# Output product of a hybrid trunk: the short convolution's second 1024 tokens through seven block products

## The chip, the cores and the metric

The program runs on one core of one Trainium2 chip. The metric is device time in microseconds of one execution of the whole kernel; less is better.

## The reference, cut to what matters

One layer over 2048 tokens of width 1024, in float32. A normalised input goes through one projection to six parts; two mixers read them; their outputs, side by side, go through one output projection `w_out` of 2048 by 1024; then an MLP follows.

```python
h = rmsnorm(x, norm_mix_w)
u_b, u_c, u_h, z, xbc, dt_raw = split(h @ w_in)          # 1024 columns each, xbc 1536, dt_raw 16
y_a = u_b * causal_dwconv(u_c * u_h, short_conv_w)       # short convolution, width 3
y_b = ssd_mixer(z, xbc, dt_raw, ...)                     # chunked state-space scan, gate, grouped norm
x = x + concat([y_a, y_b], -1) @ w_out                   # w_out: 2048 x 1024
h = rmsnorm(x, norm_mlp_w)
x = x + square(relu(h @ w_up)) @ w_down
out = rmsnorm(x, final_norm_w)
```

## The kernel before, in words

**Layout and precision.** Activations lie with features on the 128 partitions and tokens along the row. A token block is 512 tokens (`TB`), so the 2048 tokens are blocks 0 to 3; a half is 1024 tokens, two blocks. Each float32 operand is cut into a high and a low part (`uh`, `ul` for activations, `whi`, `wlo` for weights), and each product is three matmuls, high by high, high by low and low by high. A main matmul is 128 by 128 weights on 512 tokens.

**Seven products.** A product of a 2 by 2 block matrix of weights with a 2 by 2 block matrix of activations (two blocks of features by two blocks of tokens) needs eight block products the plain way, and seven with sums and differences of blocks taken first. `chain` (L267) does such a product for two column tiles of 128 outputs and one half of the tokens: seven products named b11, t1, t2, b21, t3, b22, t4, each of 4 feature tiles by 3 matmuls, 84 main matmuls in all, into three accumulators px, py and pw. Such a run is called a pair here. `after(name)` is called behind each product; it is where other work is put beside the pair. The sums of weights for the next pair are made by `combine` (L244) on VectorE; where the same columns are used for both halves, the sums of the first use are stored in DRAM and loaded at the second. The sums of activations are made where the activations come out, and are read back as seven blocks per feature tile (`land` L349, `part` L355: load into the `ul` tile, copy the high part to `uh` on ScalarE, subtract on VectorE).

**Second half** (`second_half`, L1039). Pairs 20 to 41 are the second half's input projection (`LATER`, 22 pairs; pairs 0 to 19 are the first half's). Pairs 42 to 45 (`OUTS`, o0 to o3) are the output projection of the short convolution's first half of tokens, blocks 0 and 1: y_a's seven blocks come from `y7_d`. In pair 41 the activations of the input projection are exchanged for these (`renew`), and in pair 42 the rest of them is (`renew_rest`).

**Plain units** (`Output`, L1722). The rest of the output projection is done the plain way in 48 units of one token block by one column tile, 8 feature tiles by 3 matmuls, 24 main matmuls each, accumulator pm. Pass 1 (units 0 to 15) is y_a for blocks 2 and 3, read from `ys_d`; passes 2 and 3 are y_b for blocks 0 and 2, then 1 and 3. Each unit adds its residual (`xt`, loaded from `x` in pass 1 and from `x1_d` afterwards) and stores to `x1_d`.

**The scan.** `Scan` (L1491) works through 32 chunks of 128 tokens and 8 heads. A chunk's inputs come by DMA (`load` L1518: bc, xd, dec; `load_rows`: eb; `load_gate`: y). `front` starts with TensorE transposes of xd into ptx; `back` has TensorE products st, yo, yd, then pss, and a string of VectorE steps. `run` is a generator of eight steps for a chunk, and `after` and `hook` take steps from it: chunks 0 to 21 (`SPLIT` 22) beside pairs 20 to 45, with one buffer for each chunk tile, one step behind each product, but only two steps in pair 41 and two in pair 42 (`LIGHT`); chunks 22 to 31 beside the units, with two buffers and three steps for each unit.

**Order.** On each engine, and on SP's DMA queue, instructions run in the order of the built program. A scheduler at build time sets this order from the code; nearly all DMAs are issued from SP. A transpose on TensorE whose xd has not landed holds up all matmuls behind it.

Of the kernel before, what the change touches and what calls it, by code (L numbers as in the profile page):

```python
# [16 lines left out]
P = 128  # L17
# [22 lines left out]
def trunk(ctx: ExitStack, tc: tile.TileContext, x, x_tok, w_in, w_dt, w_out, w_up, w_down, cvec, hrow, out):  # L40
# [22 lines left out]
    ys_d = dram.tile([P, 8, TH], F32, name="ys_d")  # L63
    y7_d = [dram.tile([P, 7, TB], F32, name=f"y7_d{k}") for k in range(4)]
# [147 lines left out]
    class Seven:  # L212
# [158 lines left out]
        def prepare(self, h, src, base, accs=None, held=None):  # L371
# [32 lines left out]
            for k in range(4):  # L404
                ts = [held("nb") if held and i == 1 else self.raw("nb") for i in range(4)]
# [15 lines left out]
                if held:  # L421
                    self.held.append(ts[1])
                    nc.sync.dma_start(self.stored[h][k][:, 4:6], ts[2])
# [30 lines left out]
    class Proj(Seven):  # L454
# [6 lines left out]
        OUTS = "o0 o1 o2 o3".split()  # L461
# [381 lines left out]
        def pair(self, h, what, ws, ahead, after):  # L843
# [33 lines left out]
            def evict(name, gi, pm):  # L877
# [17 lines left out]
                elif name == "b22":  # L895
# [4 lines left out]
                    elif kind == "b":  # L900
                        mul(to["c12"], to["c12"], self.cc[n][:, hi])
                        if h:
                            nc.sync.dma_start(ys_d[:, n], a)
                        else:
                            nc.sync.dma_start(y7_d[n][:, 0], to["c11"])
                            s["t13"], s["t24"] = self.e("t13"), self.e("t24")
                            self.sub(s["t13"][:, lo], to["c12"], to["c11"])
                            self.sub(s["t13"][:, hi], to["c22"], to["c12"])
                            self.sub(s["t24"][:, lo], to["c22"], s["t13"][:, lo])
                            nc.sync.dma_start(y7_d[n][:, 1:5:3], s["t13"].rearrange("p (a t) -> p a t", a=2))  # L910
# [7 lines left out]
                elif kind == "b":  # L918
                    mul(to["c21"], pm["x"], self.cc[n + 4][:, lo])
                    if h:  # L920
                        nc.sync.dma_start(ys_d[:, n + 4], b)
                    else:
                        nc.sync.dma_start(y7_d[n][:, 3:6:2], b.rearrange("p (a t) -> p a t", a=2))
                        self.sub(s["t24"][:, hi], to["c21"], s["t24"][:, lo])
                        nc.sync.dma_start(y7_d[n][:, 2:7:4], s["t24"].rearrange("p (a t) -> p a t", a=2))
# [9 lines left out]
        def residual(self, n, b):  # L935
# [3 lines left out]
            nc.sync.dma_start(t.rearrange("p (a t) -> p a t", a=2), x[b, :, 2 * n : 2 * n + 2])  # L939

        def out_pair(self, n, ws, ahead, after):
# [4 lines left out]
            def evict(name, gi, pm):  # L946
# [10 lines left out]
                if fin:  # L957
                    nc.sync.dma_start(x1_d[b][:, 2 * n + i], t)
# [3 lines left out]
        def renew(self, name):  # L962

# [1027 lines left out]
```

## Time and profile before

| | |
|---|---|
| median of 3 runs | 2608.24 us (2600.61, 2608.24, 2608.95) |
| profiled execution, its own time | 2602.47 us |
| its span, first to last instruction | 2600.5 us |
| TensorE busy | 2581.2 us of the span, 99% |
| VectorE busy | 1918.2 us, 74% |
| ScalarE busy | 1398.9 us, 54% |
| granted TensorE clock, mean | 0.999 |

Main matmuls overlap, so a row's mean duration (some 390 ns) is longer than the distance from one start to the next; what a matmul costs in a row of matmuls is read from a stretch divided by its count. In a row of the windows view stand, in this order: the stretch (us from the span's start), its length, and the busy time with the count of instructions in brackets for TensorE's matmuls, TensorE's weight loads, VectorE, ScalarE and GpSimd, then the granted TensorE clock, the DMA engines' share and GB/s. All rows are of the one profiled execution.

### The profile page before, as it was taken

How to read it: one execution, taken by the hardware profiler on the slowest of the kernel's cores; microseconds unless marked ns; L12 is line 12 of the kernel's file. 1: busy time of each engine (PE TensorE's matmuls, PEld its weight loads, DVE VectorE, ACT ScalarE, POOL GpSimd, SP SyncE). 2: the span in 40 equal slices, each digit the busy share in tenths (PEclk: the TensorE clock that was granted, in tenths of full speed). 3: DMA queues.
4: the chain of work that ended last, by engine and by line, in shares of the span. 5: the costliest groups of instructions: out<-in, count | busy, mean ns of one | idle time of the engine just before them, and what ended most of it. 6: DMA issues, size and time to landing. Idle time of an engine off the chain costs nothing.

```text
span 2600.5 us, 33553 instructions
## 1 busy us (share of the span) xinstructions
PE 2581.2 (99%) x12018; PEld 2125.3 (82%) x12018; DVE 1918.2 (74%) x2634; ACT 1398.9 (54%) x2178; POOL 65.3 (3%) x97
## 2 busy tenths in 40 slices
PE   9999999999999999999999999999999999999999
PEld 7888888788888787788888888888888888888887
DVE  7988766777777888877777765755558877877875
ACT  7554345766566865645336555655456444444443
POOL 0011000000000000000000000000000000000001
PEclk9999999999999999999999999999999999999999
DMA  5557545555555577987665674744448766676872
GB/s 214 203 206 275 199 145 190 173 170 180 163 158 185 176 255 258 281 268 234 206 220 200 238 267 142 252 161 142 161 142 283 259 205 208 222 241 219 281 251 77
DMA packets 291655, 540.23 MB, mean 208 GB/s; under 512 B 25888, under 2 KB 142112, under 8 KB 291488
## 3 DMA queue, kind: packets, MB, share of 16 engines
q1 hardware_dynamic: 291056, 537.70, 61.2%
q8 instruction: 94, 1.54, 0.2%
q14 instruction: 73, 0.60, 0.1%
q10 hardware_dynamic: 432, 0.39, 0.0%
HBM read 358.17 MB, written 179.83 MB: 207 GB/s over the span
## 4 chain that ended last, share of the span: by engine, by line
PE 70%; DMA 4%; DVE 3%; ACT 3%; issue 1%; SPq 0%; DVEq 0%; ACTq 0%
PE px L292 11%; PE px L293 11%; PE px L294 11%; PE py L292 5%; PE py L293 5%; PE py L294 5%; PE pm L132 3%; PE pm L134 3%; PE pm L133 3%; PE pw L292 3%; PE pw L293 3%; PE pw L294 3%; DMA dec<-rd_d 1%; DMA xd<-xs_d 1%; PE yd L1621 1%; PE yo L1618 1%
## 5 line engine op out<-in xcount | busy, mean ns | idle before, releaser
L292 PE MATMUL px<-uh,whi 128*128 128x512 f32 x1736 | 680.7, 392 | 2.6 <-ACT pw L300 1.5
L293 PE MATMUL px<-ul,whi 128*128 128x512 f32 x1736 | 676.3, 390 | 0.0
L294 PE MATMUL px<-uh,wlo 128*128 128x512 f32 x1736 | 675.7, 389 | 0.0
L292 PEld LDWEIGHTS px<-uh,whi 128*128 128x128 f32 x1736 | 325.9, 188 | 75.7 <-ACT pw L300 2.3
L294 PEld LDWEIGHTS px<-uh,wlo 128*128 128x128 f32 x1736 | 325.9, 188 | 68.1
L293 PEld LDWEIGHTS px<-ul,whi 128*128 128x128 f32 x1736 | 326.1, 188 | 65.7
L109 DVE TENSOR_TENSOR wlo<-wraw,whi 128x1024 fp32r<-128x1024 f32 (+1 forms) x224 | 224.8, 1003 | 193.9 <-ACT whi L108 189.9
L108 ACT CAST whi<-s 128x1024 fp32r<-128x1024 f32 (+1 forms) x214 | 223.9, 1046 | 229.9 <-PE py L293 85.2
L292 PE MATMUL py<-uh,whi 128*128 128x512 f32 x868 | 339.4, 391 | 0.0
L293 PE MATMUL py<-ul,whi 128*128 128x512 f32 x868 | 337.9, 389 | 0.0
L294 PE MATMUL py<-uh,wlo 128*128 128x512 f32 x868 | 337.9, 389 | 0.0
L108 ACT CAST whi<-wraw 128x1024 fp32r<-128x1024 f32 (+1 forms) x224 | 196.2, 876 | 245.7 <-PE px L293 168.9
L109 DVE TENSOR_TENSOR wlo<-s,whi 128x1024 fp32r<-128x1024 f32 (+1 forms) x214 | 260.4, 1217 | 73.3 <-ACT whi L108 72.1
L292 PEld LDWEIGHTS py<-uh,whi 128*128 128x128 f32 x868 | 163.0, 188 | 34.3 <-DVE state L1637 0.5
L294 PEld LDWEIGHTS py<-uh,wlo 128*128 128x128 f32 x868 | 162.9, 188 | 34.0
L293 PEld LDWEIGHTS py<-ul,whi 128*128 128x128 f32 x868 | 163.0, 188 | 33.3
L132 PE MATMUL pm<-uh,whi 128*128 128x512 f32 (+1 forms) x456 | 175.9, 386 | 0.0
L348 DVE TENSOR_TENSOR ul<-rh,uh 128x1024 fp32r<-128x1024 f32 (+1 forms) x128 | 139.0, 1089 | 49.9 <-ACT uh L347 49.8
L134 PE MATMUL pm<-uh,wlo 128*128 128x512 f32 (+1 forms) x456 | 174.0, 382 | 0.0
L133 PE MATMUL pm<-ul,whi 128*128 128x512 f32 (+1 forms) x456 | 173.4, 380 | 0.0
L347 ACT CAST uh<-rh 128x1024 fp32r<-128x1024 f32 (+1 forms) x128 | 120.2, 944 | 92.2 <-PE py L294 59.1
L292 PE MATMUL pw<-uh,whi 128*128 128x512 f32 x434 | 169.7, 391 | 0.0
(260 smaller groups left out, 3759.8 us busy)
## 6 DMA issues: line engine op xcount, KB each, us to landing
hid_d<-e SPq DMA_DIRECT2D x96, 512.0 KB, 4.0
rh<-hid_d SPq DMA_DIRECT2D x96, 512.0 KB, 4.7
wraw<-w_in SPq DMA_DIRECT2D x67, 512.0 KB, 4.4
wraw<-w_up SPq DMA_DIRECT2D x62, 512.0 KB, 4.4
wraw<-w_down SPq DMA_DIRECT2D x88, 256.0 KB, 4.3
dec<-rd_d SPq DMA_DIRECT2D x32, 512.0 KB, 5.1
wraw<-w_out SPq DMA_DIRECT2D x32, 512.0 KB, 5.1
xs_d<-cacc SPq DMA_DIRECT2D x24, 512.0 KB, 2.7
```

The lines of the kernel that those rows point to most:

```text
L108: nc.scalar.copy(hi, raw)
L109: eng.tensor_tensor(out=lo, in0=raw, in1=hi.bitcast(F32), op=ALU.subtract)
L132: nc.tensor.matmul(out, whi, hi, start=(k == 0), stop=False)
L133: nc.tensor.matmul(out, whi, lo, start=False, stop=False)
L134: nc.tensor.matmul(out, wlo, hi, start=False, stop=(k == nk - 1))
L292: nc.tensor.matmul(p, hi, h[0], start=bool(first and k == 0), stop=False, **kw)
L293: nc.tensor.matmul(p, hi, h[1], start=False, stop=False, **kw)
L294: nc.tensor.matmul(p, lo, h[0], start=False, stop=(k == len(g) - 1), **kw)
L347: nc.scalar.copy(p[i][0], t)
L348: nc.vector.tensor_tensor(out=p[i][1], in0=t, in1=p[i][0].bitcast(F32), op=ALU.subtract)
L1618: nc.tensor.matmul(yo[:, j * L : (j + 1) * L], state[:, j * P : (j + 1) * P], cT, start=True, stop=True)
L1621: nc.tensor.matmul(yd[(i % 2) * 64 : (i % 2) * 64 + 64, (i // 2) * L : (i // 2 + 1) * L], byhead(t["xdt"])[:, i, :], t["dec"][:, i, :], st ...
```

## The change

The output product of y_a's second half of tokens (blocks 2 and 3) becomes four more pairs, o4 to o7 (pairs 46 to 49), and pass 1 of the plain units goes; 32 units are left. For that: the four `b` pairs of the second half make the sums of activations too and store seven blocks (`y7_d[1]`) in place of plain y_a (`ys_d`); pair 45 (o3) and pair 46 (o4) exchange operands as pairs 41 and 42 do; o0 to o3 store the sums of weights, and o4 to o7 load them. `enter` now loads y_b of blocks 0 and 1 (with its norm weight, `cut`) where it loaded y_a of blocks 2 and 3. Of the scan, 27 chunks lie beside the pairs and 5 beside the units: each product takes one step and b11 two; the pairs that exchange operands (41, 45) take two steps at b11 and one at t2, the pairs behind them (42, 46) three, at t3, b22 and t4; the units take four steps each. In a chunk, the sum with xd moves one step forward, and with one buffer the next chunk's loads are issued one step sooner. Ahead of chunk 27's front stand two empty steps.

```diff
-    ys_d = dram.tile([P, 8, TH], F32, name="ys_d")
-    y7_d = [dram.tile([P, 7, TB], F32, name=f"y7_d{k}") for k in range(4)]
+    y7_d = [[dram.tile([P, 7, TB], F32, name=f"y7_d{h}_{k}") for k in range(4)] for h in range(2)]
...
-        OUTS = "o0 o1 o2 o3".split()
+        OUTS = "o0 o1 o2 o3 o4 o5 o6 o7".split()
...
                         mul(to["c12"], to["c12"], self.cc[n][:, hi])
-                        if h:
-                            nc.sync.dma_start(ys_d[:, n], a)
-                        else:
-                            nc.sync.dma_start(y7_d[n][:, 0], to["c11"])
-                            s["t13"], s["t24"] = self.e("t13"), self.e("t24")
-                            self.sub(s["t13"][:, lo], to["c12"], to["c11"])
...
+                        nc.sync.dma_start(y7_d[h][n][:, 0], to["c11"])
+                        s["t13"], s["t24"] = self.e("t13"), self.e("t24")
+                        self.sub(s["t13"][:, lo], to["c12"], to["c11"])
+                        self.sub(s["t13"][:, hi], to["c22"], to["c12"])
+                        self.sub(s["t24"][:, lo], to["c22"], s["t13"][:, lo])
...
+            at = 2 * (n % 4)
+            nc.sync.dma_start(t.rearrange("p (a t) -> p a t", a=2), x[n // 4 * NBB + b, :, at : at + 2])
...
+            w = w_in
             if what[0] == "o":
-                raws = self.load_cols(w_out[0], [2 * int(what[1]) + i for i in range(2)])()
-                yield
-                yield from self.combine(*raws)
-                return
-            f0, f1 = self.cols(what)
+                w, n = w_out[0], int(what[1])
+                what = f"o{n % 4}"
+                f0, f1 = 2 * (n % 4), 2 * (n % 4) + 1
+                if n < 4:
+                    sums_d[what] = dram.tile([P, 2, 1024], F32, name=f"sums_{what}_d")
+                    raws = self.load_cols(w, (f0, f1))()
+                    yield
+                    yield from self.combine(*raws, sums_d[what])
+                    return
...
+            turn = lambda m: m - nl in (-1, 3)
...
-                    if m not in (nl - 1, nl) or name in LIGHT[m - nl]:
-                        for _ in range(1 + (name == "b11" and m in DENSE)):
+                    at = m - nl
+                    rest = at in (0, 4)
+                    if name in LIGHT if turn(m) else name in LATE if rest else True:
+                        for _ in range(1 + (name == "b11")):
                             next(side, None)
...
-    SPLIT = 22
-    LIGHT = {-1: ("b11", "t2"), 0: ("b22", "t4")}
-    DENSE = ()
+    SPLIT = 27
+    LIGHT, LATE = ("b11", "t2"), ("t3", "b22", "t4")
...
                 nc.vector.tensor_tensor(out=t1, in0=yo, in1=t["eb"].rearrange("p j l -> p (j l)"), op=ALU.mult)
                 nc.vector.tensor_tensor(out=t1, in0=t1, in1=yd, op=ALU.add)
-                yield
-                nc.vector.tensor_tensor(out=t3, in0=t3, in1=t["xd"], op=ALU.add)
+                nc.vector.tensor_tensor(out=t1, in0=t1, in1=xd, op=ALU.add)
+                yield
...
+            if begin:
+                yield
+                yield
...
                     next(back)
+                    self.load(n + 1)
+                    self.load_rows(n + 1)
                     yield
                     next(back)
-                    self.load(n + 1)
-                    self.load_rows(n + 1)
                     yield
...
-        PASSES = [(0, ((2, 0), (3, 1))), (1, ((0, 2), (1, 0))), (1, ((2, 1), (3, 2)))]
-        UNITS = [(i, b, d) for i, bs in PASSES for d in range(KD) for b, _ in bs]
+        UNITS = [(b, d) for d in range(KD) for b in ((0, 1) if d < 7 else (1, 0))] + [(b, d) for d in range(KD) for b in (2, 3)]
...
+        def cut(self, b, f, o, hi, lo):
+
+            w = col(C_NSSD, f)
+            nc.scalar.mul(hi, o, w)
+            nc.vector.scalar_tensor_tensor(
+                out=lo, in0=o, scalar=w, in1=hi.bitcast(F32), op0=ALU.mult, op1=ALU.subtract
+            )
+            self.y.setdefault(b, {})[f] = hi, lo
...
             def hook(at):
-                for _ in range(1 + at % 2):
+                for _ in range(2):
                     next(side, None)
```

**On TensorE, behind pair 45 (o3).** Before, the last products of o3 (px from a `uh`/`ul` pair) and a chunk's st and yo are followed by the first plain unit, accumulator pm:

```order
L292 MATMUL px<-uh_8450,whi 128x512
L293 MATMUL px<-ul_8451,whi 128x512
L294 MATMUL px<-uh_8450,wlo 128x512
L132 MATMUL st<-xde,btok 128x512
L133 MATMUL st<-xde,btok 128x512
L134 MATMUL st<-xde,btok 128x512
L1618 MATMUL yo<-bc,state_3783 128x128 x4
L132 MATMUL pm<-uh_9076,whi 128x512
```

With the change, px of o3's last product is followed by px of o4's first product, from the newly loaded operand `uh_9382`:

```order
L291 MATMUL px<-uh_8714,whi 128x512
L292 MATMUL px<-ul_8715,whi 128x512
L293 MATMUL px<-uh_8714,wlo 128x512
L291 MATMUL px<-uh_9382,whi 128x512
L292 MATMUL px<-ul_9383,whi 128x512
L293 MATMUL px<-uh_9382,wlo 128x512
```

What moved: pm rows are replaced by rows of the seven products, and no chunk's products stand at this border any more.

**On SP's queue, the loads of the first chunk behind an exchange of operands.** Before, in pair 42 to 43: the chunk's dec, eb and xd stand behind o0's residual loads (`x<-x`) and stores (`x_d<-x`):

```order
L939 DMA x_8498<-x 128x1024
L958 DMA x_d_77<-x_8383 128x512
L958 DMA x_d_78<-x_8286 128x512
L939 DMA x_8560<-x 128x1024
L958 DMA x_d_78<-x_8286 128x512
L1529 DMA dec<-rd_d_114 128x8x128
L1552 DMA eb<-rd_d_114 64x4x128
L1527 DMA xd<-xs_d_98 128x4x128
```

With the change the same happens a second time, in pair 46 to 47, behind the loads of sums (`s<-sums_o_d`) and o4's stores:

```order
L1008 DMA s_9576<-sums_o_d 128x1024
L1009 DMA s_9577<-sums_o_d 128x1024
L933 DMA x_9584<-x 128x1024
L952 DMA x_d_79<-x_9471 128x512
L1013 DMA a_9625<-w_out 128x512
L952 DMA x_d_80<-x_9394 128x512
L933 DMA x_9658<-x 128x1024
L952 DMA x_d_80<-x_9394 128x512
L1663 DMA yn_d_102<-y 128x4x128
L952 DMA x_d_79<-x_9471 128x512
L1529 DMA bc<-xs_d_98 128x128 x2
L1531 DMA xd<-xs_d_98 128x4x128
```

What moved: a second place where xd stands behind a pair's stores, each of which waits for a VectorE addition.

**On VectorE, a chunk's sum with xd (`stmp<-stmp,xd`) and what follows.** With the change, weights and a pair's additions stand between it and the gate product `y<-stmp,y`:

```order
L1645 TENSOR_TENSOR stmp<-stmp,yd 128x512
L1646 TENSOR_TENSOR stmp<-stmp,xd 128x512
L108 TENSOR_TENSOR wlo<-wraw,whi 128x1024
L108 TENSOR_TENSOR wlo<-s_6383,whi 128x1024
L874 TENSOR_TENSOR ch<-px,s_6379 128x512
L874 TENSOR_TENSOR cc_6330<-py,s_6403 128x512
L846 TENSOR_TENSOR ch<-ch,cc_6330 128x512
L1648 TENSOR_TENSOR y<-stmp,y 128x512
```

What moved: the sum with xd frees xd's one buffer, so the next chunk's xd may be loaded from there on.

## Rows read from the trace of the kernel before

**Rows 1.** The page: busy us, share of the span, instructions of each engine.

```profile
PE 2581.2 (99%) x12018; PEld 2125.3 (82%) x12018; DVE 1918.2 (74%) x2634; ACT 1398.9 (54%) x2178; POOL 65.3 (3%) x97
```

**Rows 2.** Windows, three stretches: pairs 20 to 45; units with scan; units without.

```profile
452.05:1051.58 599.53, 592.44 (x3001) 484.49 (x3000) 460.76 (x667) 402.94 (x729) 18.22 (x39) 1.00 0.60 194
1051.58:1223.56 171.98, 169.45 (x921) 139.62 (x920) 130.73 (x208) 97.07 (x223) 0.00 (x0) 0.99 0.85 264
1223.56:1358.23 134.67, 134.67 (x613) 111.59 (x612) 93.61 (x125) 42.35 (x59) 0.00 (x0) 1.00 0.61 207
```

**Rows 3.** Windows: a bare unit, a bare pair, pairs and three units with one chunk.

```profile
1314.71:1320.15 5.44, 5.44 (x25) 4.50 (x24) 2.41 (x4) 0.58 (x1) 0.00 (x0) 1.00 0.68 224
1358.23:1377.27 19.04, 19.04 (x85) 15.77 (x84) 14.12 (x19) 13.87 (x19) 0.00 (x0) 1.00 0.60 208
756.77:779.72 22.95, 22.95 (x121) 19.10 (x120) 18.94 (x27) 13.21 (x28) 0.83 (x3) 1.00 0.45 144
779.72:802.54 22.82, 22.82 (x122) 19.02 (x120) 14.45 (x23) 11.44 (x23) 0.77 (x2) 1.00 0.53 170
1112.53:1132.74 20.21, 20.21 (x112) 16.85 (x110) 12.69 (x21) 9.32 (x23) 0.00 (x0) 1.00 0.82 248
```

**Rows 4.** Waits of TensorE, 452 to 1250 us: total, times, longest.

```profile
PE ptx L1577 <- DMA xd<-xs_d: 5.5, 6, 1.9
PE pss L1652 <- DVE ssq L1649: 1.5, 1, 1.5
PE px L292 <- ACT pw L300: 1.0, 1, 1.0
PE pss L1652 <- ACT xtok L1583: 0.9, 2, 0.5
PE st L133 <- DVE xde L1566: 0.3, 1, 0.3
PE ptx L1577 <- ACT stmp L1646: 0.2, 1, 0.2
```

**Rows 5.** Windows around the fall of the granted clock among the units.

```profile
1074.90:1097.00 22.10, 19.88 (x124) 15.95 (x123) 14.37 (x26) 15.17 (x44) 0.00 (x0) 0.96 0.88 249
1097.00:1123.00 26.00, 26.00 (x131) 21.46 (x130) 18.26 (x29) 16.37 (x38) 0.00 (x0) 0.97 0.82 248
```

**Rows 6.** The tile xd, whole span: from issue to landing.

```profile
DMA to landing us min/median/max: 2.8/4.1/5.9
```

**Rows 7.** Groups on VectorE by shape: count, busy us, mean ns, idle before.

```profile
L109 DVE TENSOR_TENSOR wlo<-s,whi 128x1024 fp32r<-128x1024 f32 x212 | 259.0, 1222 | 73.3 <-ACT whi L108 72.1 <-DMA dec<-rd_d 0.2
L231 DVE TENSOR_TENSOR e<-e 128x512 f32<-128x512 f32 x32 | 22.0, 687 | 1.4 <-DMA b_d<-e 1.3
L361 DVE TENSOR_TENSOR ul<-ul,uh 128x1024 fp32r<-128x1024 f32 x12 | 14.3, 1230 | 0.0
```

**Rows 8.** Windows of pairs 41 to 45 (z4, o0 to o3).

```profile
940.60:962.50 21.90, 21.90 (x113) 18.18 (x112) 14.93 (x20) 14.77 (x18) 0.00 (x0) 1.00 0.94 343
962.50:982.20 19.70, 19.70 (x91) 16.41 (x90) 19.16 (x24) 10.59 (x14) 0.00 (x0) 1.00 0.86 308
982.20:1006.20 24.00, 22.56 (x116) 18.28 (x115) 22.15 (x34) 14.28 (x28) 0.00 (x0) 1.00 0.84 267
1006.20:1029.70 23.50, 23.10 (x122) 18.83 (x120) 18.56 (x30) 11.77 (x25) 0.00 (x0) 1.00 0.68 231
1029.70:1051.60 21.90, 21.90 (x107) 18.13 (x105) 17.51 (x25) 17.95 (x31) 0.00 (x0) 1.00 0.93 307
```

More of the change, by code (lines that the diff above doesn't have):

```diff
@@ L404, in prepare @@
             for k in range(4):
-                ts = [held("nb") if held and i == 1 else self.raw("nb") for i in range(4)]
+                ts = [held("nb") if held and i == 2 else self.raw("nb") for i in range(4)]
                 b11, t1, t2, b21, t3, b22, t4, b12 = (t[:, i] for t in ts for i in range(2))
@@ L957, in evict, with renew @@
                 if fin:
-                    nc.sync.dma_start(x1_d[b][:, 2 * n + i], t)
+                    nc.sync.dma_start(x1_d[n // 4 * NBB + b][:, 2 * (n % 4) + i], t)
             return self.chain([self.places], ws, ahead, evict, after)
-        def renew(self, name):
+        def renew(self, h, name):
+            if name == "t1":
+                self.new = [{} for _ in range(4)]
             if name in ("t1", "b21", "b22", "t4"):
@@ L1044, in second_half @@
             nl = len(self.LATER)
-            self.new = [{} for _ in range(4)]
+            turn = lambda m: m - nl in (-1, 3)
             for m, what in enumerate(order):
                 last = m + 1 == len(order)
-                ahead = self.plain(w_out[0], (0, 1)) if last else self.weights(1, order[m + 1])
+                ahead = self.plain(w_out[1], (0, 1)) if last else self.weights(1, order[m + 1])
                 def after(name):
@@ L1814, in unit @@
             nc.sync.dma_start(x1_d[b][:, d], t)
-            if i and b < NBB:
+            if b < NBB:
                 self.square(b, d, t)
@@ L1877, in hook @@
                     f()
-            for n in range(29):
+            for n in range(13):
                 proj_out.unit(n, hook)
@@ L1882, in trunk @@
                 pass
-            for n in range(29, 32):
+            for n in range(13, 16):
                 proj_out.unit(n, hook)
@@ L1901, in hook @@
                     pass
-                mlp.got = mlp.fetch(0, 2)
+                mlp.got = mlp.fetch(0, 1)
             elif u == 30:
-                mlp.settle(mlp.places, 1, mlp.held)
-        for n in range(32, 48):
-            if n == 40:
+                mlp.settle(mlp.places, 2, mlp.held)
+        for n in range(16, 32):
+            if n == 24:
                 for tag in ("mw", "yo"):
-                    nc.tensor.matmul(psum(tag, "pw"), ones_r, proj_out.y[1, 2][0][0], start=True, stop=True)
-            if n == 46:
+                    nc.tensor.matmul(psum(tag, "pw"), ones_r, proj_out.y[2][0][0], start=True, stop=True)
+            if n == 30:
                 ahead = mlp.weights(mlp.load_cols(w_up, (0, 1)))
```

94 lines of the change are left out of this document (39 added, 55 removed).

## The prediction

> **What bounds the kernel now.** I read the page's first part, then the windows of the stretch that the change touches, then the list of what TensorE waited for, and last the tile xd. The page shows TensorE busy for 99% of the span and VectorE for 74% [rows 1]. The reader is to see that a matmul is what the time is made of: whatever takes a main matmul away takes its cost off the end, unless a wait comes in its place. The windows show where the two engines stand to each other [rows 2]: beside pairs 20 to 45 VectorE is busy 460.76 of 599.53 us, beside the units with scan 130.73 of 171.98. TensorE's idle time is 7.09 us in the first of these stretches (599.53 - 592.44) and 2.53 us in the second, none in the third. The list of waits says what it is [rows 4]: 5.5 of some 9.4 us are transposes that wait for a chunk's xd, six times, at most 1.9 us. Everything else is single waits for ScalarE or VectorE.
>
> **What it removes: main matmuls.** A bare unit takes 5.44 us for 24 matmuls and a bare pair 19.04 us for 84 [rows 3]; both make 226.7 ns a matmul (the rows count 25 and 85, since one more starts or ends at the edge). Sixteen units go, 16 x 24 = 384 matmuls, 87.0 us. Four pairs come, 4 x 84 = 336, 76.2 us. That is 48 matmuls less, **-10.9 us**. TensorE never waited in those stretches, so the price is that of TensorE at full use. The Trainium skill, page "TensorE: Matmul & The Clock Gate", section "Back-to-back issue gap", gives some 131 ns per 512-column matmul in a sustained stream, by which 48 matmuls would be worth 6.3 us. The row disagrees (226.7 ns over 84 in a row), and the row decides.
>
> **What it moves: five chunks of the scan.** A pair with a chunk takes 22.82 or 22.95 us, 3.8 to 3.9 more than a bare one; three units with a chunk take 20.21, 3.9 more than 16.32 [rows 3]. TensorE pays the same in both places: **0**. Some steps of the last chunk ran behind the pairs before; that too is only moved.
>
> **What it adds on VectorE.** Four `b` pairs get four subtractions each (16 x 0.69 us), the second exchange of operands has twelve 1024-wide and four 512-wide parts where `enter` had eight 1024-wide ones (4 x 1.23 + 4 x 0.69; the new `enter` does the scaled cuts that two blocks had in the units), the weights' low parts rise by four 1024-wide and four 512-wide ones (4 x 1.22 + 4 x 0.69), and 24 additions of pairs replace 16 of units (8 x 0.69) [rows 7]. That is 11.0 + 7.7 + 7.6 + 5.5 = 32 us more on VectorE in a stretch that gets 11 us shorter. Over the three stretches its share goes from 685 of 906 us [rows 2] to 717 of 895, from 76% to 80%. TensorE's matmuls cover it, so I cost it at **0** where it spreads out. Where it doesn't is the exchange: in pairs 42 and 43 VectorE was busy 19.16 of 19.70 and 22.15 of 24.00 us [rows 8], and TensorE idle 0 and 1.44. If that cover is gone, the price is such a pair's 1.44 us.
>
> **What it moves among the waits.** A chunk's xd took 2.8 to 5.9 us from issue to landing, 4.1 in the middle [rows 6]. The built program lists all engines in one sequence. There I counted the main matmuls between SP's load of xd and the transposes that need it. Before, 11 of 32 chunks have 12 or fewer (at most 2.7 us by 226.7 ns, so less than the landing); the usual number beside the pairs is some 20 (4.5 us). After, it is 10 of 32: the sooner load helps the chunks of the input projection (two tight ones of pairs 21 to 41 left, not counting the first two chunks), but all five chunks loaded beside o0 to o7 stand 11 matmuls behind their load, since SP's queue has stores and sums ahead of them. So the sooner load buys little: 5.5 us x 10/11, **-0.5**. The other waits of 3.9 us [rows 4] come with chunks beside pairs, 27 in place of 22: **+0.9**.
>
> At the start of the second stretch of the scan the third chunk's xd was late (1.9 us, the longest [rows 4]), and the granted clock fell right behind: 0.96 and 0.97 over two windows [rows 5] is 0.04 x 22.1 + 0.03 x 26.0 = 1.7 us lost at the lower level of 1.2 GHz. After the change that chunk has 24 matmuls of cover; but the first chunk there has 8, with SP's queue held by o7's last stores. I take half of the fall away, **-0.9**; the bounds are -1.7 and +1.7.
>
> The output pairs are the place where all this meets. Of o0 to o3, o1 had 1.44 us of idle TensorE and o2 0.40, none in the other two [rows 8], 0.46 a pair. SP's queue gets two more DMAs for sums in each of eight pairs: these are the stores and loads that xd must pass, while nothing but a chunk's front waits behind them on TensorE. For four more such pairs I add **+1.8**; the bounds are 0 and 1.44 in each of eight (11.5, less the 1.84 already there, +9.7).
>
> Sum: -10.9 - 0.5 + 0.9 - 0.9 + 1.8 = **-9.6 us**, from the profiled execution's own 2602.47 to 2592.9. The three runs lie at 2600.6, 2608.2 and 2608.9; with the profiled one their mean is 2605.1, 2.6 above it. I put the forecast on that middle: **2595.5**. Against the median of 2608.24 alone it would be 2598.6.
>
> **Rivals.**
>
> *The waits go too.* The loads are a step sooner and stand farther from their use; if xd always lands in time, the 5.5 us of xd and the 1.7 of the clock go as well, and some 1 of the rest: -19 us, 2586. For it: the usual chunk has 20 matmuls of cover, 4.5 us, against a middle landing of 4.1. Against it: ten chunks have 11 or fewer.
>
> *VectorE gives it back.* The output pairs and the units with scan become as full as pair 43. Between 42 and 49 there are two exchanges, and the chunks beside the units come at four steps a unit in place of three, each with its low parts, cuts and additions. If each of eight output pairs idles like o1, +9.7 in place of +1.8: -1.7 us, 2603, no change that shows. For it: 22.15 of 24.00 [rows 8]. Against it: pair o2, with a whole chunk, has 18.56 of 23.50, and pairs o4 to o7 make no sums of weights.
>
> *xd behind SP's queue makes it slower.* One mechanism, at the chunks beside o0 to o7 and at the first one beside the units: xd stands behind stores that wait for VectorE, it lands later than before, and each such wait lets the clock fall as it did once. The price is up to 1.9 + 1.7 = 3.6 us for each of ten tight chunks, 36 us in place of 7.2: +18 net, 2623. It ends slower (by over 0.3%) from 2.6 us a tight chunk on: (10.9 + 7.8 + 7.2) / 10. For it: DMA share 0.94 and 343 GB/s in the one exchange of before [rows 8]. Against it: the clock fell once in six waits.
>
> *A matmul is worth less than its distance.* If matmuls are held apart by something that stays when 48 go, the least that one can be worth is its weight load, 4.50 us for 24 or 187.5 ns [rows 3]: 9.0 us in place of 10.9, -7.7 with the waits, 2597.4, just too little to show. Against it: 226.7 ns is the same in bare units and bare pairs. By the page's 131 ns above it would be -5.0 us.
>
> **How the numbers follow.** Forecast 0.55, waits go too 0.16, VectorE gives it back 0.19, slower 0.08, cheap matmuls 0.02. No change means within 0.3%, 7.8 us, about what this kernel's runs can tell. Three quarters of the forecast's own case (its range is -14 to -5 us, 2591 to 2600) lie beyond that: faster 0.55 x 0.76 + 0.16 = 0.58; same 0.13 + 0.19 + 0.02 = 0.34; slower 0.08. The range goes from the second case on the lower of the runs (2600.6 - 19 = 2582) to the third on the upper ones (2608.9 - 1.7 = 2607).
>
> **What would show it.** Matmuls: 672 in the rows of px, py and pw for the output, 768 of pm, at 226.7 ns. Chunks: pairs with a chunk still near 22.9 us where nothing waits. Waits: xd at about 5 us in some six waits, most of them in pairs 46 to 49 and at the units' start, few in pairs 21 to 41. VectorE: about 32 us more busy time. If TensorE's waits between 452 and 1240 us sum to over 17 us, the third or fourth case has come; if they sum to under 3, the second. I would be wrong through a wait that no row of before shows: o4's operands, 28 blocks of 128 by 512 or 7.3 MB, that must land between the first product of o3 and the seventh of o4, or a wait on ScalarE's queue, which takes over the high parts of all this.

## The result and the profile after

The changed kernel takes 2613.86 us in the median of 16 runs (2608.84 to 2619.03), the kernel before 2602.85 in 16 runs beside them: a ratio of 1.0040, 95% interval 1.0032 to 1.0048, 10 to 11 us slower. The forecast was 2595.5, so it lies on the other side, and the time is above the range too. The profiled execution took 2610.97 us, span 2609.0.

The first line of the page, after, against [rows 1]:

```profile
PE 2577.1 (99%) x11970; PEld 2115.2 (81%) x11970; DVE 1948.6 (75%) x2674; ACT 1409.6 (54%) x2197; POOL 70.2 (3%) x97
```

TensorE has 48 matmuls fewer and is 4.1 us less busy, VectorE is 30.4 us more busy: the counts came as forecast, and the span is still 8.5 us longer. Idle time of TensorE is where to look. The windows of before and then of after are each cut into input pairs (20 to 41), output pairs (four before, eight after) and units up to the MLP; the columns are those of the rows of before:

```profile
452.05:962.48 510.43, 505.18 (x2574) 412.84 (x2573) 383.38 (x558) 348.34 (x633) 18.22 (x39) 1.00 0.56 179
962.48:1051.58 89.10, 87.27 (x429) 71.66 (x428) 77.38 (x110) 54.59 (x97) 0.00 (x0) 1.00 0.83 276
1051.58:1358.23 306.65, 304.12 (x1531) 251.21 (x1530) 224.34 (x332) 139.42 (x281) 0.00 (x0) 0.99 0.74 239
```

```profile
452.67:981.82 529.15, 517.89 (x2654) 420.63 (x2653) 415.63 (x614) 362.25 (x686) 23.26 (x39) 1.00 0.59 186
981.82:1171.43 189.61, 180.30 (x878) 145.00 (x877) 149.32 (x209) 102.52 (x179) 0.00 (x0) 0.99 0.86 297
1171.43:1368.19 196.76, 194.84 (x951) 161.14 (x950) 150.21 (x218) 88.85 (x165) 0.00 (x0) 1.00 0.76 246
```

The three stretches take 915.5 us in place of 906.2. Idle TensorE, as length less busy time: 5.25 + 1.83 + 2.53 = 9.6 us before, 11.26 + 9.31 + 1.92 = 22.5 after. So of +9.3 us, -10.9 are the products and +12.9 recorded idle time; the other 7.3 lie around the gaps and in places that I have not divided further. (A gap can cost more than its record: the one of 2.88 us at 1136 us puts the next matmul 3.04 late.) By place: the input pairs have 80 matmuls of the scan more, some 2.2 chunks, which are 8.5 us by [rows 3]; they take 18.7 us more, so they lost 10.2. The output pairs and units lost the other 10.0. This is what TensorE waited for, after, 452 to 1250 us, against [rows 4] (each line: total us, times, longest):

```profile
PE ptx L1581 <- DMA xd<-xs_d: 9.0, 7, 2.9
PE pss L1657 <- ACT xtok L1587: 4.4, 6, 1.3
PE py L291 <- ACT s L871: 2.4, 3, 0.8
PE px L291 <- DVE x L950: 1.3, 1, 1.3
PE px L291 <- ACT whi L107: 1.3, 1, 1.3
...
PE yo L1622 <- DMA bc<-xs_d: 0.8, 1, 0.8
PE px L292 <- DVE ul L360: 0.8, 2, 0.5
PE st L131 <- ACT xde L1569: 0.7, 3, 0.2
```

The list sums to 22.1 us where before it was 9.4. xd rose from 5.5 to 9.0, everything else from 3.9 to 13.1. New at the top are two waits for copies by ScalarE. `pss`, a chunk's sum of squares, waits for `xtok`, the copy of the chunk's transposed xd; that copy frees one of the two PSUM banks that `pss` shares with the transposes. `py`, an accumulator of a pair, waits for `s`, ScalarE's copy of what it held.

### The profile page after: what moved, and what is told of

Read it like the earlier page. It is cut to its first block, busy times and chain, and to the rows that moved or that the text cites. A ratio compares the mean times of both kernels' runs of the same rounds, so it can differ in the third digit from the quotient of the medians.

```text
span 2609.0 us, 33614 instructions
## 1 busy us (share of the span) xinstructions
PE 2577.1 (99%) x11970; PEld 2115.2 (81%) x11970; DVE 1948.6 (75%) x2674; ACT 1409.6 (54%) x2197; POOL 70.2 (3%) x97
## 4 chain that ended last, share of the span: by engine, by line
PE 57%; DMA 5%; DVE 2%; ACT 1%; issue 1%; SPq 0%; DVEq 0%; ACTq 0%
PE px L291 9%; PE px L292 9%; PE px L293 9%; PE py L293 5%; PE py L291 5%; PE py L292 5%; PE pw L293 2%; PE pw L291 2%; PE pw L292 2%; PE pm L131 2%; PE pm L133 2%; PE pm L132 2%; DMA ul<-y_d 1%; DMA dec<-rd_d 1%; DMA xd<-xs_d 1%
## 5 line engine op out<-in xcount | busy, mean ns | idle before, releaser
L291 PE MATMUL px<-uh,whi 128*128 128x512 f32 x1800 | 706.6, 393 | 2.8 <-DVE x L950 1.3
L292 PE MATMUL px<-ul,whi 128*128 128x512 f32 x1800 | 702.2, 390 | 0.9 <-DVE ul L360 0.8
L293 PE MATMUL px<-uh,wlo 128*128 128x512 f32 x1800 | 700.7, 389 | 0.0
L291 PEld LDWEIGHTS px<-uh,whi 128*128 128x128 f32 x1800 | 338.0, 188 | 79.5 <-issue 3.3
L291 PE MATMUL py<-uh,whi 128*128 128x512 f32 x900 | 352.8, 392 | 2.4 <-ACT s L871 2.4
L293 PE MATMUL py<-uh,wlo 128*128 128x512 f32 x900 | 350.8, 390 | 0.3 <-DVE wlo L108 0.3
L292 PE MATMUL py<-ul,whi 128*128 128x512 f32 x900 | 350.5, 389 | 0.0
L293 PE MATMUL pw<-uh,wlo 128*128 128x512 f32 x450 | 175.9, 391 | 0.0
L292 PE MATMUL pw<-ul,whi 128*128 128x512 f32 x450 | 175.6, 390 | 0.0
L299 ACT COPY pw<-px 128x512 f32<-128x512 f32 x118 | 67.6, 573 | 117.3 <-PE px L293 117.1
```

The source lines that it names most:

```text
L291: nc.tensor.matmul(p, hi, h[0], start=bool(first and k == 0), stop=False, **kw)
L292: nc.tensor.matmul(p, hi, h[1], start=False, stop=False, **kw)
L293: nc.tensor.matmul(p, lo, h[0], start=False, stop=(k == len(g) - 1), **kw)
L299: self.copied = nc.scalar.copy(pm[gi]["w"], pm[gi]["x"]).ins
```

## The experiments

All runs in one table: median us, ratio to the kernel before on the same chip with its 95% interval, and TensorE's idle us in the windows above (input pairs / output pairs / units) of the one profiled execution. The runs are of several chips, on which the kernel before took 2602.9 to 2606.6 us in the median, and single profiles of a kernel differ by a few us; so the verdicts are the ratios'. Each expectation below names the theories that the text then speaks of; a letter belongs to the expectations around it and is not carried further.

| run | us | ratio (interval) | idle |
|---|---|---|---|
| before | 2602.9 | 1 | 5.2 / 1.8 / 2.5 |
| changed | 2613.9 | 1.0040 (1.0032-1.0048) | 11.3 / 9.3 / 1.9 |
| e1 loads as before | 2613.9 | 1.0030 (1.0019-1.0042) | 13.9 / 8.8 / 1.1 |
| e2 pss apart | 2624.2 | 1.0069 (1.0056-1.0082) | 16.4 / 9.7 / 2.8 |
| e3 second step at t3 | 2617.4 | 1.0040 (1.0028-1.0052) | 14.0 / 9.6 / 0.3 |
| e5 before, eight steps | 2613.7 | 1.0025 (1.0014-1.0036) | 9.6 / 0.0 / 2.5 |
| f2 before, no scan | 2471.6 | 0.9486 (0.9474-0.9498) | 0.0 / 0.6 / 0.0 |
| f3 changed, no scan | 2467.2 | 0.9470 (0.9458-0.9482) | 0.4 / 5.9 / 0.0 |
| g1 f3, sums by ScalarE | 2463.3 | 0.9449 (0.9436-0.9462) | 0.0 / 3.5 / 0.0 |
| f5 changed, xd ahead | 2615.5 | 1.0040 (1.0027-1.0053) | 15.2 / 6.7 / 0.5 |
| f6 before, xd ahead | 2606.1 | 1.0000 (0.9992-1.0009) | 4.6 / 2.1 / 4.6 |
| g2 changed, sums by ScalarE | 2612.0 | 1.0024 (1.0015-1.0034) | 15.6 / 8.8 / 0.7 |
| g3 changed, xd on GpSimd | 2621.1 | 1.0054 (1.0041-1.0067) | 16.6 / 10.2 / 1.3 |
| g4 both of these | 2619.4 | 1.0049 (1.0035-1.0063) | 16.7 / 10.1 / 1.6 |
| h1 changed, decays behind copy | 2607.6 | 1.0006 (0.9998-1.0015) | 5.8 / 8.0 / 1.0 |
| h2 g2 and h1 | 2606.1 | 0.9998 (0.9990-1.0007) | 5.5 / 10.3 / 1.1 |
| h5 seven steps in input pairs | 2617.8 | 1.0048 (1.0035-1.0061) | 7.6 / 12.0 / 6.4 |
| h6 same, nine in output pairs | 2620.4 | 1.0053 (1.0041-1.0065) | 8.4 / 14.7 / 5.3 |
| k1 before, decays behind copy | 2602.9 | 0.9987 (0.9978-0.9996) | 5.0 / 2.5 / 4.7 |
| k2 h2 and f5 | 2594.6 | 0.9954 (0.9942-0.9967) | 3.1 / 4.9 / 2.3 |

**Which part costs: the eighth step, the loads, or the output pairs?** The eighth step alone, put into the kernel before:

```diff
-    SPLIT = 22
+    SPLIT = 24
...
-                        for _ in range(1 + (name == "b11" and m in DENSE)):
+                        for _ in range(1 + (name == "b11")):
```

> The kernel before with eight steps a pair (two behind b11) and 24 chunks beside the 26 pairs instead of 22; its output products and loads unchanged. Kernel before: 2602.9 us, TensorE's waits from 452 to 1240 us 9.6. Theory A (eight steps to eight fix the phase): waits for ScalarE's copies xtok and s appear, 3 to 7 us, time 2605 to 2611. Theory B (the cost is in the new output pairs): within 2 us of the kernel before.

Slower by 0.25%, some 6.5 us (interval 3.6 to 9.4), and the first three waits are the first three of the changed kernel:

```profile
PE pss L1652 <- ACT xtok L1583: 3.7, 3, 2.2
PE ptx L1577 <- DMA xd<-xs_d: 3.2, 4, 1.5
PE py L292 <- ACT s L872: 2.5, 3, 0.8
```

The input pairs take 527.7 us in place of 510.4 with the same 2.2 chunks more, 8.5 us: the eighth step loses 8.8 there (in the changed kernel 10.2), and gets some 3 back where output pairs and units have fewer chunks. Theory A held, and the output pairs alone (theory B) can't be the whole of it.

The loads and the sum with xd put back to where they were, in the changed kernel:

```diff
+                yield
                 nc.vector.tensor_tensor(out=t1, in0=t1, in1=xd, op=ALU.add)
-                yield
...
                     next(back)
-                    self.load(n + 1)
-                    self.load_rows(n + 1)
                     yield
                     next(back)
+                    self.load(n + 1)
+                    self.load_rows(n + 1)
                     yield
```

> The changed kernel with a chunk's loads and the sum with xd where the kernel before has them (the load one step later, xd added in the step of the gate); all else as changed. Changed kernel: 2613.9 us, kernel before 2602.9. Theory A (a pair now has eight steps, a chunk has eight, so every chunk meets ScalarE's busiest stretch at the same place, and the copy xtok that frees a PSUM bank is late; the loads matter little): pss still waits 3 to 5 us in all for xtok, time 2611 to 2617. Theory C (the sooner loads let the decay's eight activations go ahead of the copy on ScalarE): the pss waits fall under 1.5 us, xd waits grow by 1 to 6 us, time 2606 to 2612. Theory B (the four new output pairs are what costs): within 2 us of the changed kernel.

1.0030 against 1.0040, intervals overlapping; `pss` waits 7.0 us for `xtok`, not under 1.5 (and more than theory A's 3 to 5). The sooner loads are not what costs, and buy nothing that shows. Theory C fell.

The doubled step moved to another product:

```diff
-                        for _ in range(1 + (name == "b11")):
+                        for _ in range(1 + (name == "t3")):
```

> The changed kernel with a pair's second step behind the product t3 instead of b11; still eight steps a pair, 27 chunks. Theory A (the place at which a chunk's steps meet a pair's work decides): TensorE's waits from 452 to 1240 us, 22.5 us in the changed kernel, move by more than 4 us either way, with other releasers than xtok; time 2605 to 2622. Theory D (any place meets a ScalarE that is busy 22 to 24 us of a convolution pair's 24 to 25): waits of 20 to 25 us, time within 3 us of 2613.9.

The same ratio, and the idle TensorE of the three stretches is 23.9 us for 22.5: by its numbers theory D's case. But it is not ScalarE that is late:

```profile
PE ptx L1581 <- DMA xd<-xs_d: 15.0, 19, 2.3
PE px L291 <- DVE x L950: 3.1, 4, 1.7
PE px L293 <- DVE wlo L108: 2.3, 3, 1.2
```

`pss` hardly waits (0.2 us), and the transposes wait 19 times. So the place of the steps decides who waits, and this place is as dear: neither theory had it whole.

`pss` taken out of the transposes' banks:

```diff
-            pss = psum("tp", "pss", 2) if self.bufs == 1 else psum("mw", "pss", accs["mw"])
+            pss = psum("yo", "pss") if self.bufs == 1 else psum("mw", "pss", accs["mw"])
```

> The changed kernel, with the sum of squares pss in the PSUM bank of yo instead of the two banks that it shares with the transposes; nothing else differs in the code. Theory A: the six waits of pss for ScalarE's copy xtok (4.4 us, 5.3 us with what each gap costs beyond its idle time) go, time down by 4 to 6 us, to 2608 to 2610. Rival: pss then waits for ssq, or the next transposes wait for the same copy, and at least half of the 4.4 us comes back under another name: time within 2 us of 2613.9.

A miss: the `pss` waits went, and the kernel became 7.5 us slower. `yo` now waits for `pss`'s reader (1.2 us), `st` for `xde` (3.2), and the transposes for xd 15.4 us in 11 gaps. A part of the loss is the clock: the mean granted clock of e2's six runs is 0.9972, of the changed kernel's 16 runs 0.9986, and 0.0014 of the span is 3.7 us. A bank changes the order of all instructions, and I did not settle which of the waits came first.

**Is it the output pairs alone?** Both kernels with the work of the chunks left out (each chunk loads its gate and stores it):

```diff
...
+                for _ in range(7):
+                    yield
+                nc.sync.dma_start(yn_d[h][:, 4 * g : 4 * g + 4, ts], y)
```

> The kernel before with the work of the scan's chunks left out: each chunk only loads its gate and stores it in the place of its result, at the same steps. 32 chunks at 3.9 us beside pairs and units are 125 us, with their waits 10 more: about 2470 to 2480 us. It is the base for the next run.

> The changed kernel with the same work left out. Arithmetic theory (48 products fewer are worth 226.7 ns each, and all that the change loses is lost to the chunks): 9 to 12 us under the kernel before without the scan. Theory B (the four new output pairs and their exchange lose it themselves, with no chunk beside them): less than 5 us under it, or none.

The change is worth -4.4 us there in place of -10.9, so theory B holds for a part. The windows of the output pairs and of the units, first before, then changed, both without scan:

```profile
884.42:962.16 77.74, 77.16 (x338) 62.79 (x336) 56.79 (x70) 32.53 (x40) 0.00 (x0) 1.00 0.75 252
962.16:1224.64 262.48, 262.48 (x1160) 217.45 (x1158) 141.32 (x181) 73.22 (x93) 0.00 (x0) 1.00 0.70 232
```

```profile
884.77:1046.43 161.66, 155.81 (x673) 125.21 (x672) 107.05 (x131) 68.28 (x84) 0.00 (x0) 1.00 0.88 307
1046.43:1221.87 175.44, 175.44 (x775) 145.36 (x774) 111.81 (x146) 54.12 (x70) 0.00 (x0) 1.00 0.72 235
```

The last 18 input pairs take 19.04 us each in both, and it is mostly o0 and o1 that lose (22.5 and 22.3 us), waiting for VectorE and ScalarE. SyncE's queue shows a reason (start us, us, the DMAs issued; first before, then changed):

```profile
885.07 0.32 SPq L899 DMA_DIRECT2D sz_d<-ea  x1
885.48 1.72 SPq L353 DMA_DIRECT2D ul<-y_d  x3
887.30 0.38 SPq L917 DMA_DIRECT2D sz_d<-eb  x1
887.77 2.54 SPq L353 DMA_DIRECT2D ul<-y_d  x4
890.40 1.72 SPq L100 DMA_DIRECT2D wraw<-w_out  x2
```

```profile
886.11 0.32 SPq L898 DMA_DIRECT2D sz_d<-ea  x1
887.37 0.32 SPq L262 DMA_DIRECT2D sums_o_d<-s  x1
887.78 2.61 SPq L352 DMA_DIRECT2D ul<-y_d  x4
890.44 0.47 SPq L913 DMA_DIRECT2D sz_d<-eb  x1
891.00 4.13 SPq L352 DMA_DIRECT2D ul<-y_d  x4
897.02 1.69 SPq L99 DMA_DIRECT2D wraw<-w_out  x2
```

The store of a kept weight sum, `sums_o_d<-s`, can't go until VectorE has the sum, and the loads of the output product's operands `ul<-y_d` stand behind it: their last is issued by 895.1 us where it was 890.3. The test is to send those eight stores by another queue:

```diff
-                nc.sync.dma_start(kept[:, 0], s12)
+                (nc.scalar if queue else nc.sync).dma_start(kept[:, 0], s12)
...
-                    yield from self.combine(*raws, sums_d[what])
+                    yield from self.combine(*raws, sums_d[what], True)
```

> The changed kernel without the scan's work (2467.2 us; the kernel before without it 2471.6), with the eight stores of the kept weight sums of o0 to o3 issued by ScalarE's queue in place of SyncE's; nothing else. Theory S (the store of a sum stands at the head of SyncE's queue until VectorE has the sum, and the loads of the output product's inputs stand behind it: in the run above eight of them are issued from 887.8 to 895.1 us, in the kernel before from 885.5 to 890.3): TensorE's waits in the output pairs, 5.9 us, fall by 3 to 5 and the time to 2462 to 2465. Theory V (VectorE is simply full there, 18 of 22 us): within 1.5 us of 2467.2.

-3.9 us by the medians, the time that theory S gave; by the ratios it is 5.5, with intervals that overlap at their ends. The output pairs take 158.3 us in place of 161.7, though their recorded idle time fell by 2.3 and not by 3 to 5. The change is now worth 2463.3 - 2471.6 = -8.3 us without scan, with 2.9 us more idle TensorE than f2.

> The changed kernel, whole, with the same edit. Theory S, with nothing given back: 3 to 6 us less, 2608 to 2611 where the changed kernel is at 2614. Rival (a wait that goes in one place comes back at the next chunk, as when xd was loaded ahead): within 2 us of 2614.

1.0024 for 1.0040, some 4 us by the ratios (the intervals overlap at their ends) and 2 by the medians, which are of different chips: likely theory S's gain, less sure than without scan.

**Is xd what it all ends in?** ScalarE writes the scaled xd into `xtok`'s tile, so that xd's own tile is free sooner and is loaded then:

```diff
...
+            xd = t["xd"]
+            if self.bufs == 1:
+                t["xd"] = xtok.rearrange("p (j l) -> p j l", j=4)
             for j in range(4):
-                nc.scalar.mul(t["xd"][:, j], t["xd"][:, j], col(C_D, 4 * g + j))
+                nc.scalar.mul(t["xd"][:, j], xd[:, j], col(C_D, 4 * g + j))
...
                     next(front, None)
+                    self.load_xd(n + 2)
                     yield
```

> The changed kernel, in which ScalarE writes the scaled xd into xtok's tile, which is idle then, so that xd's tile comes free a part of a chunk sooner and the next chunk's xd is loaded right then, not behind VectorE's sum. Theory E (every stall upstream ends in the one xd tile: VectorE's sum, then 2.8 to 5.9 us of landing, then the transposes): the xd waits of 9.0 us go to under 1.5, and with 0.2 us more of each gap the time falls by 7 to 12 us, to 2602 to 2607. Theory A (ScalarE's queue and the phase of eight steps): the chunk then stalls at pss and py instead, waits of 7 us remain or grow, time 2609 to 2614.

> The kernel before with the same edit. Its xd waits are 5.5 us in six gaps: by theory E 5 to 8 us faster than the kernel before, 2595 to 2599 where that is at 2603; by theory A within 3 us of it.

Neither kernel moved, although no transpose waits for xd any more in f5. The waits came back in other places; the first four of f5:

```profile
PE pss L1669 <- ACT xtok L1596: 5.8, 6, 2.4
PE pss L1669 <- DVE ssq L1666: 3.7, 3, 1.6
PE px L292 <- DVE ul L360: 2.7, 2, 1.5
PE pss L1669 <- ACT pw L299: 2.6, 2, 1.5
```

Theory E fell in this form: 12.1 us of `pss` stand where 9.0 of xd stood.

**Is ScalarE too full?** Its four scalings of xd go to GpSimd:

```diff
+                dskip = cv[:, C_D + 4 * g : C_D + 4 * g + 4].unsqueeze(2).to_broadcast([P, 4, L])
+                nc.gpsimd.tensor_tensor(out=t["xd"], in0=t["xd"], in1=dskip, op=ALU.mult)
```

> The changed kernel with the four scalings of xd of the 27 chunks beside pairs done by one operation on GpSimd, which is idle there, in place of four on ScalarE (393 ns each, some 1.3 us a chunk). Theory A (ScalarE, 22 to 24 us of a convolution pair's 24 to 26, is what comes late once each pair has a whole chunk): the waits for ScalarE's xtok, s, whi, xde (8.8 us in the changed kernel) fall by 3 us or more, time 2606 to 2611. Rival (VectorE is late as much; GpSimd's operation makes VectorE's slower, and the sum with xd waits for it): 2612 to 2620.

> Both edits. By theories S and A together 7 to 11 us less than the changed kernel, 2603 to 2607, where it meets the kernel before; by their rivals 2612 to 2620.

By the ratios 0.14% slower than without in g3, where the intervals overlap, and 0.25% in g4, where they just don't; in g3 `pss` still waits 7.4 us for `xtok`. The input pairs of g3:

```profile
452.86:989.60 536.74, 520.12 (x2654) 421.47 (x2653) 427.75 (x613) 337.01 (x596) 52.93 (x62) 1.00 0.58 183
```

ScalarE is 25 us less busy there than in the changed kernel, VectorE 12 us more, with the same work. So less work for ScalarE did not help. As VectorE became slower at the same time, this run alone doesn't rule out that ScalarE is too full; h1 below points to its order instead, with no work taken off it. The Trainium skill, page "SBUF — State Buffer", section "Who interferes with whom", has GpSimd and VectorE share one pair of SBUF ports, which one of them locks against the other. The 12 us, beside 22 GpSimd products of 1.06 us in the middle, agree with that; no run here shows the lock itself.

**Is it the order on ScalarE?** The tile `pss` between 560 and 960 us, before and then changed, with what its engine sat idle for (us and times, the weight load's share included):

```profile
  ACT xtok L1583: 2.7, 4
```

```profile
  ACT xtok L1587: 12.2, 14
```

And ScalarE's timeline at one of these waits in the changed kernel; the chunk's transposes end at 770.4, `pss` is due at 773:

```profile
768.03 0.99 ACT L1601 ACTIVATE dec<-dec,dd 128x128 f32<-128x128 f32 x3 [1.81 <-DMA dec<-rd_d]
768.93 1.03 ACT L107 CAST whi<-s 128x1024 fp32r<-128x1024 f32 x1
769.86 1.57 ACT L1601 ACTIVATE dec<-dec,dd 128x128 f32<-128x128 f32 x5
771.34 0.61 ACT L107 CAST whi<-a 128x512 fp32r<-128x512 f32 x1
771.85 1.06 ACT L121 ACTIVATE dec<-dec 128x1024 f32<-128x1024 f32 x1
772.81 1.13 ACT L836 ACTIVATE cc<-ch,cv 128x1024 f32<-128x1024 f32 x1
773.85 0.56 ACT L1587 COPY xtok<-ptx 128x512 f32<-128x512 f32 x1
```

ScalarE first stands still until the load of the decays `dec` has landed, then does all eight and their exponential, 4 us with what lies between, and only then the copy. Both kernels have that order in most chunks: in the traces all eight decays stand ahead of the copy in 15 of the first 22 chunks, before and after. The code has the decays two steps behind the copy, and the scheduler pulled them ahead. What differs is when they come: from the end of the chunk's last transposes (`ptb`) to the end of the copy it is 1.1 us in the median of chunks 5 to 20 before and 2.6 after, and `pss` is due at 2.6. Before, the eight steps of a chunk took 8/7 of a pair, 26 us; now they take one pair, 23, and the decays come closer to the transposes. The test orders the decays behind the copy:

```diff
-            nc.scalar.copy(xtok, pt)
+            copied = nc.scalar.copy(xtok, pt).ins if self.bufs == 1 else None
...
             for i in range(HG):
-                relu = nc.scalar.activation(dec[:, i], dec[:, i], AF.Relu, bias=t["a"][:, i : i + 1], scale=-1.0)
+                with behind(copied):
+                    relu = nc.scalar.activation(dec[:, i], dec[:, i], AF.Relu, bias=t["a"][:, i : i + 1], scale=-1.0)
```

> The changed kernel with ScalarE's eight decay activations of a chunk ordered behind its copy xtok, beside the pairs; nothing else. Theory O (order on ScalarE: the decays wait at the head of its queue for their load and take 4 us, and the copy that frees pss's bank stands behind them): the six waits of pss for xtok (4.4 us) go under 1 us; time 2607 to 2611. Theory N (one chunk in each pair of 22.9 us leaves its loop, from yd over the loads, transposes, copy, decays and back, no slack; what is removed at one place is met at the next): pss stops waiting and xd, s, yd or dec wait in its place, time 2611 to 2618.

1.0006 for 1.0040, intervals apart: 9 us back by this order alone. The copy ends 0.6 us behind the transposes, the input pairs' idle time is 5.8 us, and `pss` no longer waits for `xtok`; from the list of waits:

```profile
PE ptx L1581 <- DMA xd<-xs_d: 6.1, 5, 3.6
PE px L291 <- DVE x L950: 2.5, 2, 1.3
...
PE pss L1660 <- DVE ssq L1657: 0.2, 1, 0.2
```

Theory O held, N did not.

> The kernel before with the decays ordered behind the copy xtok, as in the run that gave the changed kernel 9 us back. If what that edit mends came with the change (pss waits 0.9 us for xtok in the kernel before, 4.4 in the changed one), it does little here: within 3 us of the kernel before. If it is a gain of its own, that any kernel with these chunks would have: 5 us or more below it.

Between the two: 0.9987, so 3.4 us of the nine are a gain that the kernel before can have as well; some 5.5 came with the change. The profiles point the same way: the input pairs, where `pss` waited, take 522.3 us in h1 for 529.2, and 510.0 in k1 for 510.4.

> The changed kernel with both edits, the kept sums' stores on ScalarE's queue (2612.0, 6.3 us over the kernel before) and the decays behind the copy. Theory O: 2604 to 2608, level with the kernel before. Theory N: 2609 to 2615.

0.9998: both mended places together bring the changed kernel level with the one before, as theory O had it. What the stores add to h1's 1.0006 is not clear of noise, and against k1, the kernel before with the same order, h2 is 0.11% slower, with intervals that overlap.

**Fewer steps in the input pairs in place of that?** With the sums' stores as in g2, and the operands of token block 2 loaded two units later:

```diff
...
-                        for _ in range(1 + (name == "b11")):
+                        for _ in range(1 + (name == "b11" and at >= -1)):
...
-    SPLIT = 27
+    SPLIT = 24
...
-            put(2, 2, 14, (18, 20, 22, 24))
+            put(2, 2, 18, (22, 24, 26, 28))
...
-                for _ in range(2):
+                for _ in range(3):
                     next(side, None)
```

> The changed kernel with the kept sums' stores on ScalarE's queue and seven steps in each input pair (eight in the output pairs), so 24 chunks beside pairs, and eight of them beside units at three steps a half unit. Theory N or any by which the eighth step in the input pairs costs the 10 us: the input pairs lose what they did in the kernel before (TensorE's waits there 5 us, 15.6 with eight steps), time 2600 to 2606. Rival (the work must go somewhere: the first 13 units are 102 us with some 100 us of VectorE work, so that VectorE holds them up): waits of 5 to 15 us among the units, time 2608 to 2620.

> As the run before, with nine steps in five output pairs, 25 chunks beside pairs and seven beside units. Theory N: 2599 to 2606, input pairs as before, output pairs up to 5 us more waits. Rival: the output pairs, where VectorE is busy 150 of 190 us, lose it: 2608 to 2620.

Their rivals held (h6 ends 0.4 us above its range). The input pairs' idle time does fall to 7.6 and 8.4 us, but the chunks put beside the units and the fuller output pairs lose it there (12.0 + 6.4, 14.7 + 5.3).

**And what is left?** In h2 the xd waits are 11.3 us in seven gaps. All three edits (g2's, h1's and f5's) together:

> The changed kernel with three edits: kept sums' stores on ScalarE's queue, decays behind the copy, and the next chunk's xd loaded as soon as ScalarE has scaled the last one into xtok's tile. Alone that third edit gave nothing, and the waits came back at pss (12.1 us). If that was ScalarE's order again, the xd waits left with the first two edits (11.3 us in 7 gaps) now go without a return: 2594 to 2600, under both kernels. If what is removed in one place is met in the next: 2604 to 2610.

0.9954, 11.5 us under h2 and 12 under the kernel before, the fastest of those with the scan. Its first waits:

```profile
PE pss L1672 <- DVE ssq L1669: 1.8, 3, 1.0
PE px L291 <- DVE x L950: 1.7, 1, 1.7
PE px L291 <- ACT uh L359: 1.3, 1, 1.3
```

xd is gone from the list, and this time nothing of its size took its place: the other waits are 9.8 us in all where h2 had 5.3. As f5's edit alone gave nothing, what had taken its gain was mended by h1's and g2's edits; that it was h1's order on ScalarE is likely, since f5's waits stood at `pss`, but the two were not tried apart. The clock has a part in it too: the mean granted clock of the runs is 0.9985 in h2 and 0.9996 in k2, 2.9 us of the 11.5.

## Why the prediction was wrong

**The products, -10.9: right.** Without scan the units take 262.48 - 175.44 = 87.04 us less, and o2, o4, o5 and o6, which wait for nothing there, take 19.04 to 19.06 us, 76.2 for four: -10.9. With the stores out of the way (g1) the change is worth -8.3 us, and idle TensorE differs by 2.9: -11.2. The Trainium skill, page "TensorE: Matmul & The Clock Gate", section "Back-to-back issue gap", gives 131 ns a matmul, by which it would be an estimated 6.3 us. The measured windows don't agree with it; they agree with 226.7 ns.

**The moved chunks, 0: right where nothing waits.** Pairs with a chunk and no wait take 22.94 us after, as in [rows 3].

**VectorE's 32 us, 0: the work was right (30.4), and without scan it was hidden in the input pairs; beside o0 and o1 it was not.** In f3 VectorE has 8 us more to do in the input pairs than in f2, and they take 0.6 us longer.

**"The other waits of 3.9 us come with chunks beside pairs, 27 in place of 22: +0.9": this step failed.** It scaled the waits of before by the number of chunks. They rose to 13.1 us, and e5, h1 and k1 show the largest new one: the steps of a chunk moved against each other. Eight steps to a pair in place of seven took 3 us out of the loop of a chunk, and a copy that had come 1.5 us before its use came at it. The row was in sight: `pss <- ACT xtok`, 0.9 us, twice [rows 4], is a hand-over that in some chunks has no time left. The text's last sentence named ScalarE's queue as what could make it wrong, and gave it no chance and no price. Ordering the decays behind the copy gave 9 us back, 5.5 of them the change's own.

**Output pairs, +1.8: mis-sized.** The output pairs and units lost 7.8 us without any scan (337.1 us in f3's two windows, 340.2 in f2's, and -10.9 was due). "SP's queue gets two more DMAs for sums in each of eight pairs" was there, priced for what xd loses behind them; the operands of o0 and o1 stood behind them too, which is some 3.9 of the 7.8 us (g1). The rest is for the most part waits for VectorE, in o0, o1 and o7, that no run took away.

**xd, -0.5 and the clock, -0.9: wrong sign for the one, nothing for the other.** xd rose from 5.5 to 9.0 us. The seven waits are four beside the input pairs (3.6 us) and three beside output pairs (5.4). In the profile the clock fell once again, behind the longest of them, the 2.9 us of o6. The windows there (as in [rows 5]):

```profile
1134.00:1138.00 4.00, 1.64 (x11) 1.45 (x11) 1.65 (x4) 3.07 (x11) 0.00 (x0) 0.97 1.07 347
1138.00:1152.00 14.00, 14.00 (x57) 11.51 (x56) 10.46 (x15) 7.05 (x14) 0.00 (x0) 0.89 0.72 256
```

0.03 x 4.0 + 0.11 x 14.0 is 1.7 us, what it was before. Over all runs the mean granted clock is 0.9986 in the changed kernel and 0.9991 to 0.9994 in the kernel before on the other chips, so 1 to 2 us of the loss are the clock's. The fourth case (xd behind SP's queue) named a mechanism that is there and costs little: the loads of o1 and o5 were issued 4.7 and 9.8 us after the sum that frees their tile, and the transposes then waited 0 and 0.3 us. The two long waits, 2.2 and 2.9 us, are for loads that were issued 0.1 and 0.9 us after that sum and took 4.4 and 5.2 us to land; there the sum itself came late for the transposes, and why is open. The price of 3.6 us for each of ten chunks was too high. The sign that the text set, waits of over 17 us, came true: 22.1.

What stays open: 7.3 us around the gaps were not divided; why e2 lost 7.5 us is not settled; and the kernel before with k2's edits of the scan was not run, so I can't say how much of k2's 12 us is the change's own. Against k1, the kernel before with one of them, k2 is 8.6 us faster by the ratios; f5's edit on top of k1 could take some of that away.

## What to carry to other kernels

Packing side work more densely does not scale its waits; it shifts them. Before a step is added per block, look at each hand-over in the loop of the side work (here transposes, copy, `pss`) for how much time is left between ready and due, and take a wait of 0.9 us as a sign that there is none. A store that needs a result not yet computed must not stand in the queue that feeds the next product. And a mended wait that gives nothing (f5) is not a dead end: on top of the other two edits it was worth 11.5 us.

## What the runs showed of the hardware

GpSimd's product of 128x512 took 1.06 us in the middle and 2.1 at most, and with 27 such products moved to it VectorE was busy 13 us longer for the same work (1961.8 us in place of 1948.6). The granted clock fell to its lower level, 1.2 GHz, behind the wait of 2.88 us in the changed kernel and not behind the one of 2.17 us at 1060 us, while before it fell behind 1.9 us: the length of a wait alone does not tell it. It has a price: the mean granted clock of the runs was 0.9970 to 0.9973 in e2, h5 and h6 and 0.9996 in k2, which is 6 to 7 us of their span.
